# Loading the first slab in four parts and storing the middle slabs whole in a FiLM layer

## The chip, the cores and the metric

The kernel runs on one core of a Trainium2 chip. The metric is the device time of one execution in microseconds (us), lower is better. A core has a tensor engine (PE), a vector engine (DVE), a scalar engine (ACT), GpSimd (POOL) and a sync engine (SP). In this kernel SP and ACT issue the transfers, each to its own queue, and 16 DMA engines carry out both queues. The trace calls SP's queue q1 and ACT's q10. "SPq" and "ACTq" are the instruction streams of these engines where they issue transfers.

## The reference

```python
batch, seq, dim, cond_dim = 32, 512, 256, 64
gamma = conditioning @ gamma_proj            # [32, 64] @ [64, 256]
beta  = conditioning @ beta_proj
out   = x * (1 + gamma[:, None, :]) + beta[:, None, :]     # x, out: [32, 512, 256] float32
```

Two small products give each batch entry a scale and a shift for each of 256 features, and every one of the 512 sequence rows of that entry is scaled and shifted by them. x and out have 16.78 MB each, and each is moved once. Everything is float32.

## The kernel before

**Tiling.** x is seen as 4 slabs of 8 batch entries (4.19 MB). In a slab, partition p holds 32 consecutive rows of 256 features: 32 KB in one contiguous run, in HBM as in SBUF. So 16 neighbouring partitions belong to one batch entry, and each partition needs one row of gamma and one of beta. All four slabs have a tile of their own (`xs0` to `xs3`), which is updated in place and stored from; no buffer is used twice.

**Loads.** ACT first issues the three small loads: conditioning into `cond_s` (L48), gamma_proj and beta_proj into the two halves of `gbproj` (L50, L51). SP issues the loads of x (L59), in the order of the slabs, as the table `LOADS` (L38) says: slab 0 in two DMAs, of 8 and of 24 rows of each partition, every other slab in one DMA of 32 rows. A DMA of n rows consists of 128 runs of n KB, one for each partition.

**Scale and shift.** An identity repeated 16 times along its columns (`rident`, L67) is multiplied with conditioning (L72), which gives its transpose with each column repeated for the 16 partitions of a batch entry. It goes to SBUF (`cond_T`, L74). For each slab one product with `gbproj` (L79) gives gamma and beta for each partition in PSUM (`gb_p`). ACT copies them to SBUF as `gb_s`, with 1 added to gamma (L82, L85).

**The main loop.** It runs over the slabs, and in a slab over two groups of 16 rows. DVE takes 11 rows of a group and reads gamma and beta from PSUM: L100 does (gamma + 1) * x, L103 adds beta. POOL takes the other 5 rows and reads the SBUF copies: L102 multiplies, L104 adds. When both have finished with a group, ACT issues its store (L105), 16 rows of each partition, 2.10 MB. The tile framework places the semaphores, and orders each engine's instructions; POOL runs the multiplications of both groups of slab 0 before its additions.

**Order.** Each engine works through its instructions in order, and each of the two DMA queues takes its transfers in the order of issue. The stores stand on ACT behind the copies to `gb_s`.

Of the kernel before, what the change touches and what calls it, by code (L numbers as in the profile page):

```python
# [2 lines left out]

# [5 lines left out]


@with_exitstack
def kernel(
    ctx: ExitStack,
    tc: tile.TileContext,
    x: bass.AP,
    conditioning: bass.AP,
    gamma_proj: bass.AP,
    beta_proj: bass.AP,
    out: bass.AP,  # L20
):
    nc = tc.nc
    f32 = mybir.dt.float32
    ALU = mybir.AluOpType

    batch, seq, dim = x.shape
    cond_dim = conditioning.shape[1]
    P = 128
    SLABS = 4
    BS = batch // SLABS  # L30
    REP = P // BS
    ROWS = BS * seq // P
    assert SLABS * BS == batch and REP * BS == P and ROWS * REP == seq

    x_v = x.flatten_outer_dims().rearrange("(s p r) d -> s p r d", s=SLABS, p=P)
    o_v = out.flatten_outer_dims().rearrange("(s p r) d -> s p r d", s=SLABS, p=P)

    LOADS = {0: [8, 24]}  # L38
    GROUP = 16
    ON_DVE = 11  # L40

    consts = ctx.enter_context(tc.tile_pool(name="consts", bufs=1))
    xpool = ctx.enter_context(tc.tile_pool(name="xpool", bufs=1))
    psum = ctx.enter_context(tc.tile_pool(name="psum", bufs=1, space=bass.MemoryType.PSUM))


    cond_s = consts.tile([batch, cond_dim], f32)
    nc.scalar.dma_start(out=cond_s, in_=conditioning)  # L48
    gbproj = consts.tile([cond_dim, 2 * dim], f32)
    nc.scalar.dma_start(out=gbproj[:, :dim], in_=gamma_proj)  # L50
    nc.scalar.dma_start(out=gbproj[:, dim:], in_=beta_proj)  # L51

    slabs = []
    for s in range(SLABS):
        xs = xpool.tile([P, ROWS, dim], f32, name=f"xs{s}")
        slabs.append(xs)
        r = 0
        for n in LOADS.get(s, [ROWS]):
            nc.sync.dma_start(out=xs[:, r : r + n, :], in_=x_v[s, :, r : r + n, :])  # L59
            r += n  # L60
        assert r == ROWS


    ident = consts.tile([batch, batch], f32)
    make_identity(nc, ident)
    rident = consts.tile([batch, batch * REP], f32)
    nc.vector.tensor_copy(  # L67
        out=rident.rearrange("p (b g) -> p b g", g=REP),
        in_=ident.to_broadcast([batch, batch, REP]),
    )  # L70
    cond_T_p = psum.tile([cond_dim, batch * REP], f32)
    nc.tensor.matmul(cond_T_p, lhsT=cond_s, rhs=rident, start=True, stop=True)  # L72
    cond_T = consts.tile([cond_dim, batch * REP], f32)
    nc.vector.tensor_copy(out=cond_T, in_=cond_T_p)  # L74

    gb_p, gb_s = [], []
    for s in range(SLABS):
        p_t = psum.tile([P, 2 * dim], f32, name=f"gb_p{s}")
        nc.tensor.matmul(p_t, lhsT=cond_T[:, s * P : (s + 1) * P], rhs=gbproj,  # L79
                         start=True, stop=True)  # L80
        s_t = consts.tile([P, 2 * dim], f32, name=f"gb_s{s}")
        nc.scalar.activation(out=s_t[:, :dim], in_=p_t[:, :dim],  # L82
                             func=mybir.ActivationFunctionType.Identity,
                             bias=1.0, scale=1.0)
        nc.scalar.copy(out=s_t[:, dim:], in_=p_t[:, dim:])  # L85
        gb_p.append(p_t)
        gb_s.append(s_t)

    def rows(t, n):
        return bass.AP(tensor=t.tensor, offset=t.offset, ap=[t.ap[0], [0, n], t.ap[1]])  # L90

    for s in range(SLABS):
        xs = slabs[s]
        g_p, b_p = gb_p[s][:, :dim], gb_p[s][:, dim:]
        g_s, b_s = gb_s[s][:, :dim], gb_s[s][:, dim:]
        for r0 in range(0, ROWS, GROUP):
            v = xs[:, r0 : r0 + ON_DVE, :]
            w = xs[:, r0 + ON_DVE : r0 + GROUP, :]
            nv, nw = ON_DVE, GROUP - ON_DVE
            nc.vector.scalar_tensor_tensor(out=v, in0=rows(g_p, nv), scalar=1.0, in1=v,  # L100
                                           op0=ALU.add, op1=ALU.mult)
            nc.gpsimd.tensor_tensor(out=w, in0=w, in1=rows(g_s, nw), op=ALU.mult)  # L102
            nc.vector.tensor_add(out=v, in0=v, in1=rows(b_p, nv))  # L103
            nc.gpsimd.tensor_tensor(out=w, in0=w, in1=rows(b_s, nw), op=ALU.add)  # L104
            nc.scalar.dma_start(out=o_v[s, :, r0 : r0 + GROUP, :],  # L105
                                in_=xs[:, r0 : r0 + GROUP, :])


# [1 line left out]
_INS = ['x', 'conditioning', 'gamma_proj', 'beta_proj']  # L110
_OUTS = [((32, 512, 256), 'float32')]


# [23 lines left out]
```

## Time and profile before

| | |
|---|---|
| Median of 5 runs | 84.53 us (84.29 to 84.71) |
| The profiled execution | 84.53 us, its span 82.7 us |
| DVE busy | 49.9 us (60%) |
| POOL busy | 46.2 us (56%) |
| PE, ACT busy | 9.1 us, 3.9 us |
| Moved by DMA | 33.69 MB, mean 407 GB/s over the span |
| Small loads to landing | cond 3.2 us, gamma 9.2 us, beta 13.0 us |
| Eight stores to landing | 18.8 us, the median from issue |

The span runs from the first instruction of the core to the last; the rest of the time lies outside it. The busy shares are those of the engines. The page also has two rows in 40 equal slices, for the engines and for the DMA engines, in tenths (9 is 90% or more). In a row of a DMA queue the columns are packets, MB, and the time of the packets as a share of 16 engines in the stretch that was asked for. A packet is counted in the stretch in which it starts, so that shares of short stretches can be a little over 100%. In this kernel a packet of x is one run of one partition: the loads of 8, 24 and 32 rows have packets of 8, 24 and 32 KB.

### The profile page before, as it was taken

The numbers are of one execution on the slowest core, as the hardware profiler recorded it, in microseconds if no ns is written. First come the engines' busy times: TensorE is split into PE (matmuls) and PEld (weight loads), VectorE is DVE, ScalarE is ACT, GpSimd is POOL, SyncE is SP. The second block draws the span as 40 slices with busy tenths as digits, with TensorE's granted clock in tenths as the row PEclk, the third lists the DMA queues.
The fourth block names the chain that finished last, engine by engine and source line by source line (L and its number), as shares of the span: only waits on it lengthen the run. The fifth ranks groups of instructions, "written<-read, shape, count | busy, mean of one in ns | idle before, by whom it ended". The sixth has DMA issues, their size and how long they took to land.

```text
span 82.7 us, 156 instructions
## 1 busy us (share of the span) xinstructions
PE 9.1 (11%) x10; PEld 2.8 (3%) x10; DVE 49.9 (60%) x18; ACT 3.9 (5%) x9; POOL 46.2 (56%) x22
## 2 busy tenths in 40 slices
PE   0090000899600000000000000000000000000000
PEld 0000000443000000000000000000000000000000
DVE  2002000049999999999999999999999920000000
ACT  0600000034400000000000000000000000000000
POOL 2000000059999999999999999999995000000000
DMA  2899999989969989898989969999999999999992
GB/s 48 309 543 396 388 396 523 396 364 507 507 285 475 507 364 380 364 523 380 396 380 507 491 285 467 404 451 436 412 452 404 451 436 412 452 404 459 428 412 95
DMA packets 2080, 33.69 MB, mean 407 GB/s; under 512 B 288, under 2 KB 416, under 8 KB 416
## 3 DMA queue, kind: packets, MB, share of 16 engines
q1 hardware_dynamic: 720, 16.78, 48.6%
q10 hardware_dynamic: 1360, 16.92, 47.9%
HBM read 16.92 MB, written 16.78 MB: 407 GB/s over the span
## 4 chain that ended last, share of the span: by engine, by line
DVE 48%; DMA 16%; issue 11%; PE 2%; ACTq 1%; ACT 1%
DVE xs L100 30%; DVE xs L103 19%; DMA gbproj<-in_beta_proj_dram 16%; PE gb_p L79 2%; ACTq L50 1%; ACTq L48 0%; ACT gb_s L82 0%; ACT gb_s L85 0%
## 5 line engine op out<-in xcount | busy, mean ns | idle before, releaser
L102 POOL TENSOR_TENSOR xs<-xs,gb_s 128x1280 f32<-128x1280 f32 x8 | 23.0, 2889 | 16.3 <-ACT gb_s L82 16.3
L100 DVE SCALAR_TENSOR_TENSOR xs<-gb_p,xs 128x2816 f32<-128x2816 f32 x8 | 24.7, 3084 | 10.9 <-ACT gb_s L85 10.9
L103 DVE TENSOR_TENSOR xs<-xs,gb_p 128x2816 f32<-128x2816 f32 x8 | 24.7, 3087 | 0.3
L104 POOL TENSOR_TENSOR xs<-xs,gb_s 128x1280 f32<-128x1280 f32 x8 | 23.0, 2890 | 0.0
L79 PE MATMUL gb_p<-gbproj,cond_T 64*128 64x512 f32 x8 | 7.2, 1073 | 8.9 <-DMA gbproj<-in_beta_proj_dram 8.9
L74 DVE COPY cond_T<-cond_T_p 64x512 f32<-64x512 f32 x1 | 0.7, 683 | 4.5 <-PE cond_T_p L72 4.5
L79 PEld LDWEIGHTS gb_p<-gbproj,cond_T 64*128 64x128 f32 x8 | 2.5, 326 | 13.6 <-issue 13.6
L72 PE MATMUL cond_T_p<-rident,cond_s 32*64 32x512 f32 x2 | 1.9, 1065 | 4.1 <-DMA cond_s<-in_conditioning_dram 4.1
L82 ACT ACTIVATE gb_s<-gb_p 128x256 f32<-128x256 f32 x4 | 1.5, 384 | 16.5 <-PE gb_p L79 16.5
L85 ACT COPY gb_s<-gb_p 128x256 f32<-128x256 f32 x4 | 1.5, 366 | 0.0
L82 ACT ACT_TABLE_LOAD x1 | 1.3, 1283 | 2.4 <-issue 2.4
L67 DVE COPY rident<-ident 32x512 f32<-32x512 f32 x1 | 0.4, 415 | 1.2 <-POOL ident masks.py:199 1.2
L72 PEld LDWEIGHTS cond_T_p<-rident,cond_s 32*64 32x64 f32 x2 | 0.3, 202 | 4.0 <-issue 4.0
masks.py:197 POOL MEMSET ident<- 32x32 f32 x1 | 0.1, 114 | 0.3 <-POOLq L121 0.3
masks.py:199 POOL TENSOR_SCALAR_AFFINE_SELECT ident<-ident 32x32 f32<-32x32 f32 x1 | 0.2, 203 | 0.1
L121 POOL MEMSET const-float32-0.0<- 128x1 f32 x1 | 0.1, 104 | 0.2 <-issue 0.2
L121 POOL MEMSET const-bfloat16-1.0<- 128x1 bf16 x1 | 0.1, 107 | 0.0
L121 POOL MEMSET const-uint8-127<- 128x1 uint8 x1 | 0.1, 107 | 0.0
L121 POOL MEMSET const-float32-1.0<- 128x1 f32 x1 | 0.1, 104 | 0.0
## 6 DMA issues: line engine op xcount, KB each, us to landing
out_dram<-xs ACTq DMA_DIRECT2D x8, 2048.0 KB, 18.8
xs<-in_x_dram SPq DMA_DIRECT2D x3, 4096.0 KB, 33.1
xs<-in_x_dram SPq DMA_DIRECT2D x1, 3072.0 KB, 12.4
xs<-in_x_dram SPq DMA_DIRECT2D x1, 1024.0 KB, 4.8
gbproj<-in_gamma_proj_dram ACTq DMA_DIRECT2D x1, 64.0 KB, 9.2
gbproj<-in_beta_proj_dram ACTq DMA_DIRECT2D x1, 64.0 KB, 13.0
cond_s<-in_conditioning_dram ACTq DMA_DIRECT2D x1, 8.0 KB, 3.2
```

The lines of the kernel that those rows point to most:

```text
L50: nc.scalar.dma_start(out=gbproj[:, :dim], in_=gamma_proj)
L67: nc.vector.tensor_copy(out=rident.rearrange("p (b g) -> p b g", g=REP), in_=ident.to_broadcast([batch, batch, REP]),)
L72: nc.tensor.matmul(cond_T_p, lhsT=cond_s, rhs=rident, start=True, stop=True)
L74: nc.vector.tensor_copy(out=cond_T, in_=cond_T_p)
L79: nc.tensor.matmul(p_t, lhsT=cond_T[:, s * P : (s + 1) * P], rhs=gbproj, start=True, stop=True)
L82: nc.scalar.activation(out=s_t[:, :dim], in_=p_t[:, :dim], func=mybir.ActivationFunctionType.Identity, bias=1.0, scale=1.0)
L85: nc.scalar.copy(out=s_t[:, dim:], in_=p_t[:, dim:])
L100: nc.vector.scalar_tensor_tensor(out=v, in0=rows(g_p, nv), scalar=1.0, in1=v, op0=ALU.add, op1=ALU.mult)
L102: nc.gpsimd.tensor_tensor(out=w, in0=w, in1=rows(g_s, nw), op=ALU.mult)
L103: nc.vector.tensor_add(out=v, in0=v, in1=rows(b_p, nv))
L104: nc.gpsimd.tensor_tensor(out=w, in0=w, in1=rows(b_s, nw), op=ALU.add)
L121: nc = _bacc.Bacc("TRN2", target_bir_lowering=False, num_devices=1)
```

## The change

Two tables of the kernel are changed, and the store at the end of the loop follows the new one.

- `LOADS` gives slab 0 four DMAs of 8 rows each, where it had one of 8 and one of 24. SP issues seven loads of x and not five.
- `STORES` gives the rows at which a slab's stores end. Slabs 0 and 3 are stored in two halves as before. Slabs 1 and 2 are stored by one DMA of 32 rows, 4.19 MB, after their second group. ACT issues six stores and not eight.

The lines that issue the three small loads are not touched. The arithmetic, its groups and its split between DVE and POOL are the same.

```diff
-    LOADS = {0: [8, 24]}
+    LOADS = {0: [8, 8, 8, 8]}
+    STORES = {0: (16, 32), 1: (32,), 2: (32,), 3: (16, 32)}
     GROUP = 16
     ON_DVE = 11
...
             nc.gpsimd.tensor_tensor(out=w, in0=w, in1=rows(b_s, nw), op=ALU.add)
-            nc.scalar.dma_start(out=o_v[s, :, r0 : r0 + GROUP, :],
-                                in_=xs[:, r0 : r0 + GROUP, :])
+            done = r0 + GROUP
+            if done in STORES[s]:
+                e0 = 0
+                for e1 in STORES[s]:
+                    if r0 < e1 <= done or STORES[s] == (ROWS,):
+                        nc.scalar.dma_start(out=o_v[s, :, e0:e1, :], in_=xs[:, e0:e1, :])
+                    e0 = e1
```

## The prediction

> **What bounds the kernel now.** I read the page first: engine shares, the row of DMA busy tenths, the queues.
>
> ```profile
> span 82.7 us, 156 instructions
> PE 9.1 (11%) x10; PEld 2.8 (3%) x10; DVE 49.9 (60%) x18; ACT 3.9 (5%) x9; POOL 46.2 (56%) x22
> DMA  2899999989969989898989969999999999999992
> q1 hardware_dynamic: 720, 16.78, 48.6%
> q10 hardware_dynamic: 1360, 16.92, 47.9%
> ```
>
> DVE and POOL are busy for a little over half the span. The 16 DMA engines have no empty slice between the first and the last, and the two queues' shares add to 96.5%. Queue q1 carries the x loads from SP; q10 carries the stores and the three small loads from ACT (16.92 MB is 16.78 of stores and 0.14 of small loads).
>
> Next the chain of waits, the timeline and the DMA issues, to see whether compute could be what ends last.
>
> ```profile
> 1.72 13.04 DMA gbproj<-in_beta_proj_dram
> 17.43 2.90 POOL L102 TENSOR_TENSOR xs<-xs,gb_s 128x1280 f32<-128x1280 f32 x1 [16.30 <-ACT gb_s L82]
> 26.07 0.37 ACTq L105 DMA_DIRECT2D out_dram<-xs  x1
> 30.06 0.34 ACTq L105 DMA_DIRECT2D out_dram<-xs  x1
> 66.80 0.34 ACTq L105 DMA_DIRECT2D out_dram<-xs  x1
> out_dram<-xs ACTq DMA_DIRECT2D x1, 2048.0 KB, 15.1
> ```
>
> The chain names beta's load (13.04 us), which holds back all arithmetic until 17.4 us. That chain is true for DVE, but DVE does not set the end. The last store is issued at 66.80 and lands 15.1 us later, at 81.9. One store of 2.10 MB needs about 4.9 us of the engines (64 packets of 0.61 us per engine make eight stores: 39 us), so some 10 us of that are a queue of earlier stores. The end is set by bytes over DMA rate: an earlier start of the arithmetic buys nothing unless the DMA engines would have been empty.
>
> So the price list is that of the packets. I asked for the DMA view in stretches with one kind of packet each: 3 to 4.7 us (8 KB loads), 5.2 to 9.5 (24 KB loads beside gamma), 15.12 to 22.3 (32 KB loads), 50 to 80 (16 KB stores), 28.4 to 33.8 (loads and stores). The columns are packets, MB, share of 16 engines.
>
> ```profile
> q1 hardware_dynamic: 86, 0.70, 97.7%
> ...
> q1 hardware_dynamic: 64, 1.57, 85.8%
> q10 hardware_dynamic: 64, 0.07, 4.3%
> ...
> q1 hardware_dynamic: 96, 3.15, 101.4%
> ...
> q10 hardware_dynamic: 881, 12.86, 100.1%
> ...
> q1 hardware_dynamic: 48, 1.57, 77.1%
> q10 hardware_dynamic: 32, 0.52, 22.6%
> ```
>
> Share times 16 engines times the stretch, over packets, gives one packet on one engine: 8 KB 0.309 us; 24 KB 0.922; 32 KB 1.213; 16 KB stores 0.612 (of the 881, 96 are 4-byte completion packets, which I leave out). Per KB they are 0.0386, 0.0384, 0.0379 and 0.0383: within 2%. The row of loads and stores together is the exception: between 28.4 and 33.8 us a 32 KB load took 0.771 x 16 x 5.4 / 48 = 1.388 us, while the stores beside it kept 0.612. That dip cost (1.388 - 1.213) x 48 / 16 = 0.5 us per engine.
>
> **The change, part by part.** The sum is made against the profiled execution: 84.53 us with a span of 82.7, so 1.8 us lie outside. It equals the median of the five runs (84.53; 84.29 to 84.71). A change under about 0.3%, 0.25 us, can't be told from none.
>
> *Slab 0 as four loads of 8 rows instead of 8 and 24.* Each engine carries 8 partitions, one packet each: 8 packets of 8 KB and 8 of 24 KB become 32 of 8 KB. Added: 24 x 0.309 = 7.42 us. Removed: 8 x 0.922 = 7.38. Net +0.04. This lies on the path, as all DMA time does. SP issues two more DMAs, 0.36 to 0.43 us each in the trace (one took 0.70); the engines have the first 8-row load to work on from 1.7 us and need 2.5 us for each, so the issues are hidden. If that cover were gone, 0.4 us each would show.
>
> A rule speaks against this part. The Trainium skill, "DMA: Bandwidth & Descriptors", section Bandwidth, gives 341 GB/s for a 1 MB transfer measured alone and 425 for 16 MB, and its fit charges about 2.0 us fixed per DMA. Two more DMAs would be +4 us by that (an estimate from the page). The trace differs: the 3 to 4.7 us row moves 0.70 MB of 8 KB loads at 97.7% of the engines, and the seam between slab 0's two loads, at 4.8 us, lies in the third slice of the page's DMA row, which reads 9. With the next load already queued the fixed part is covered, so I charge 0.04 and not 4; the page's price would hold only if SP came late.
>
> *The small loads.* The diff does not move their issue: cond, gamma and beta still leave ACT at 0.74, 1.17 and 1.72. What changes is what they alternate with. In the 5.2 to 9.5 row, 64 x packets go with exactly 64 gamma packets: one for one. Gamma and beta have 4 packets per engine and a completion each, so ten turns. A turn costs 0.92 + 0.05 us beside 24 KB packets and 0.31 + 0.05 beside 8 KB ones. From about 5 us, ten turns of 0.36 bring beta home near 9 us (my estimate, 7 to 9.5), not 14.76. POOL and DVE then start near 11.8 instead of 17.5. The bytes are the same, so on the path this is worth 0; its cover is the DMA queue itself.
>
> *Slabs 1 and 2 stored whole.* For these slabs 32 packets of 16 KB per engine become 16 of 32 KB. No row shows a 32 KB store. The bounds are twice the 16 KB one (1.224) and the load of that size (1.213): 0 to -0.17 us. Halfway, -0.08. ACT issues two DMAs fewer (0.34 us each), hidden, as ACT has nothing else by then. Each whole store waits for both halves of its slab, so the first half goes out some 6 us later (DVE's four 3.09 us instructions per slab). Queued behind it on ACT are only the stores of later slabs, which are ready later anyway.
>
> *Does the queue run dry?* This is what would break the sum. With slab 0 starting near 11.8, its two stores issue near 20.3 and 24.3 (8.6 and 12.6 us after POOL's start, as in the timeline). Before, q10 has no packet from 28.4 to 29.7 us, so the first store packet came about 3.7 us after its issue at 26.07; now writing begins near 24. From there each engine alternates 32 KB loads with 16 KB stores; before, from 34.5 to 49 us, this ran at about 287 and 142 GB/s (4.16 and 2.06 MB in 14.5 us). Slab 2 has about 0.65 MB by then; the other 3.5 MB at 287 GB/s bring it home near 36.5, and 4.2 MB more bring slab 3 home near 51 (before, the last load landed 39.3 us after its issue at 10.43, so at 49.7). Slab 1 landed 21.6 us after its issue at 1.63, and does so again. DVE, at 12.25 us a slab, ends slab 0 at 24.2, slab 1 at 36.4, slab 2 at 48.8, slab 3 at 63.3. When loads end, the store queue still holds the tail of slab 0 and all of slab 1; slab 2 joins at 48.8. At 4.9 us per 2.1 MB these last to about 71, while slab 3's halves are ready at 59.7 and 63.3. That leaves about 8 us of margin after the 3.7 us. What is late next is nothing.
>
> Sum: +0.04 - 0.08 = -0.04 us. 84.53 - 0.04 = 84.5.
>
> **The rivals.**
>
> *The mixed stretch costs more (slower).* The only large loss of before is the dip of 0.5 us, in loads, just as the first store joined them. If reading slab 2 while writing slab 0 is what costs, it now lasts longer: before, three load packets per engine met it; now slab 0's writing covers the last six or seven. At 0.175 us each that is +0.5 to +0.7 us: 85.1. It decides from two more slow packets per engine (0.35 us). For it: the slow loads appear together with the stores. Against it: from 34.5 us on loads and stores ran together at full pace, and store packets were never slow; the five runs' spread of 0.42 us is as large as such a dip, so it may be chance.
>
> *The dips go (faster).* A smaller one is the first round of slab 1, at 12.5 to 13.9 us, when packets of 32 KB took some 1.34 us. If these dips belong to the old order of transfers (24 KB runs, first stores at 29.8 us), up to 0.6 us comes back: 83.9. Against it: nothing in the trace names a cause.
>
> *A load issued late (slower).* The fifth x load was held 7.6 us by gamma:
>
> ```profile
> SPq L59 <- DMA gbproj<-in_gamma_proj_dram: 7.6, 1, 7.6
> ```
>
> A completion counter is used again there. Seven x loads now need more of them, and a wait of slab 2's load is bounded by the landings ahead of it. If slab 2's load waited for slab 1's landing (about 23 us) the engines would empty at 22 and refill about 1 us after the issue: +2 us, 86.6. It decides from a release after 22 us. Against it: a counter of an early, small transfer is the natural one to come free, and gamma was. And that the change does nothing as its words say (no small load is moved on its queue) gives the forecast's time again.
>
> **How the numbers follow.** Unchanged within 0.3%: 0.46. Mixed stretch: 0.27. Dips gone: 0.22. Late load: 0.05. So faster 0.22, same 0.46, slower 0.32; the likeliest time is 84.5, its own range 84.25 to 84.8. To 8 in 10 I take in most of the first two rivals: 83.95 to 85.3. The late load and the outer part of the dips stay out.
>
> **What would show it.** Right: beta landing near 9 us and the arithmetic starting near 12, yet the end near 81.9; DMA tenths of 8 and 9 throughout; six stores, the last issued near 63 and landing some 18 us later instead of 15.1. Packets of 0.309 us for 8 KB, and 1.21 to 1.22 for the 32 KB stores. The first rival: load packets of 1.4 us over more of 24 to 37 us. The second: no such stretch. The third: an empty slice near 22 us and a wait of SP on a load of x. Wrong altogether: a slice under 8 tenths late in the span, before the last store is issued.

## The result, and the profile after

The changed kernel takes 84.05 us (median of 27 runs, 83.90 to 85.62) against 84.53 us (48 runs). The ratio is 0.9962, with a 95% interval of 0.9948 to 0.9975: faster by 0.25 to 0.52%. A second set of runs, with runs of before beside them, gave 0.9942 (0.9914 to 0.9969). Of the kernels below, those with stores of 8 rows, two loads of 16, one delay and the other slab order were profiled in a disturbed execution, so their load packets are not read here.

The page of the changed kernel, first the span and the DMA rows, then the issues with their time to landing:

```profile
span 83.0 us, 155 instructions
DMA  3899999979969999896999989799699979899980
q1 hardware_dynamic: 1008, 16.78, 48.2%
q10 hardware_dynamic: 1072, 16.92, 47.6%
...
out_dram<-xs ACTq DMA_DIRECT2D x2, 4096.0 KB, 23.9
gbproj<-in_beta_proj_dram ACTq DMA_DIRECT2D x1, 64.0 KB, 7.6
```

The DMA engines are full from end to end, as before. Beta lands after 7.6 us instead of 13.0. The profiled execution took 84.78 us, more than the median and more than before, with a span 0.3 us longer than before's 82.7. A wrong conclusion is easy here. Share times span gives the time an engine spends on packets, on average over the 16: 40.0 us of loads and 39.5 of stores after, 40.2 and 39.6 before. The engines had less to do, yet the end came later: the last store issued at 65.58 and landed 16.6 us later, at 82.2, and one engine's completion packet is the only DMA packet after 81.5 us. In the second profile of the same kernel (84.33 us) nothing is left after 81.5. One late engine sets the end of an execution, so the sums over all 16 engines are a steadier guide than the span.

The timeline after, for the answer to the lines of before:

```profile
20.64 0.37 ACTq L111 DMA_DIRECT2D out_dram<-xs  x1
24.63 0.34 ACTq L111 DMA_DIRECT2D out_dram<-xs  x1
38.10 3.09 DVE L101 SCALAR_TENSOR_TENSOR xs<-gb_p,xs 128x2816 f32<-128x2816 f32 x1 [1.31 <-DMA xs<-in_x_dram]
53.16 3.09 DVE L101 SCALAR_TENSOR_TENSOR xs<-gb_p,xs 128x2816 f32<-128x2816 f32 x1 [2.73 <-DMA xs<-in_x_dram]
65.58 0.34 ACTq L111 DMA_DIRECT2D out_dram<-xs  x1
out_dram<-xs ACTq DMA_DIRECT2D x1, 2048.0 KB, 16.6
```

The stores start 5.4 us earlier than before. DVE now waits for slabs 2 and 3, 1.31 and 2.73 us in brackets, which costs nothing: the last store still waits behind others, 16.6 us where its own bytes need 4.9.

Where the time came from is in the load packets where the stores join. The rows of one stretch, 23 to 38 us, are, in order: before, after, after a second time.

```profile
q1 hardware_dynamic: 160, 4.72, 76.3%
...
q1 hardware_dynamic: 144, 4.19, 65.7%
...
q1 hardware_dynamic: 146, 4.23, 66.6%
```

MB over 32 KB gives the 32 KB packets: 144, 128 and 129 (the rest of the count are completion packets). An undisturbed one takes 1.213 us. Before, an engine spent 0.763 x 15 = 11.45 us on 9 packets that should take 10.92: 0.53 us too much. After, the same working gives 0.15 and 0.21. So 0.3 to 0.4 us of slow loads are gone, most of the gain of 0.3 to 0.5 us.

A smaller stretch of slow loads is gone too, the first round of slab 1. Here are its rows, before from 12.5 to 13.0 us, then after from 12.7 to 13.4:

```profile
q1 hardware_dynamic: 32, 0.52, 269.1%
q10 hardware_dynamic: 30, 0.03, 18.2%
...
q1 hardware_dynamic: 36, 0.56, 185.6%
```

Both hold 16 packets of 32 KB, besides completion packets and, after, four packets of 8 KB. They took 1.34 us each before and 1.21 after, which is 0.12 us less per engine. Before, beta's last packets (q10) are still under way; after, beta has landed by then. Of the kernels below, stores alone and beta behind slab 0 also have beta under way there, and their first round took 1.32 and 1.39 us. In loads alone, and with gamma and beta early, beta has landed, and it took 1.21.

The slow packets do not stand in one place even in the changed kernel. The rows of 23.1 to 27 us and of 27 to 36 us are, for the first profile and then for the second:

```profile
q1 hardware_dynamic: 32, 1.05, 64.8%
q1 hardware_dynamic: 80, 2.62, 67.9%
...
q1 hardware_dynamic: 32, 1.05, 62.3%
q1 hardware_dynamic: 80, 2.62, 69.5%
```

A load packet took 1.26 and then 1.22 us in the first, 1.21 and then 1.25 us in the second, though the first store packet came at 24.1 and 24.8 us.

### The profile page after: what moved, and what is told of

It reads as the page before. It is cut to its first block, busy times and chain, and to the rows that moved or that the text cites. A ratio compares the mean times of both kernels' runs of the same rounds, so it can differ in the third digit from the quotient of the medians.

```text
span 83.0 us, 155 instructions
## 1 busy us (share of the span) xinstructions
PE 9.1 (11%) x10; PEld 2.8 (3%) x10; DVE 50.1 (60%) x18; ACT 3.9 (5%) x9; POOL 46.3 (56%) x22
## 4 chain that ended last, share of the span: by engine, by line
DMA 62%; DVE 15%; ACTq 1%; issue 0%; DVEq 0%
DMA xs<-in_x_dram 53%; DMA gbproj<-in_beta_proj_dram 9%; DVE xs L104 7%; DVE xs L101 7%; ACTq L51 1%; ACTq L49 0%; DVEq L101 0%
```

## The experiments

Theory A said that fewer and longer store packets gained, B that the loads gained, through the slow load packets where the stores join, C that it was spread. Each ratio is to runs of before made beside it.

**Loads alone.** Against the changed kernel:

```diff
-    STORES = {0: (16, 32), 1: (32,), 2: (32,), 3: (16, 32)}
+    STORES = {s: (16, 32) for s in range(SLABS)}
```

> Slab 0 in four loads of 8 rows, all slabs stored in halves as before. Theory A (fewer, longer store packets are what gained): no gain here, +0.04 us by the prediction's packet prices, 84.5 to 84.6. Theory B (the loads gained: beta lands near 9.3 us, the stores begin near 24 us instead of 29.8, and the stretch of slow loads at that point shrinks): most of the 0.48 us, 84.0 to 84.2, with the load packets between 23 and 29 us near 1.25 us instead of 1.39. Theory C (the gain is spread of runs): ratio between 0.998 and 1.002 here and in the store-only kernel.

Its load row in 23 to 38 us:

```profile
q1 hardware_dynamic: 144, 4.19, 65.6%
```

That is 0.14 us of slow loads, as after: the mechanism of B. The time did not follow at once: the ratio was 0.9984 (0.9945 to 1.0022), inconclusive; the profiled execution took 84.36 us. Its end shows a cost of another kind. Its last store lands at 64.33 + 17.2 = 81.5 us, 0.4 earlier than before, but its span ends 1.05 us after that, where before and after need 0.8. The end of the program, line L138, between 81.5 and 81.9 us, in this kernel:

```profile
64.33 0.34 ACTq L111 DMA_DIRECT2D out_dram<-xs  x1
out_dram<-xs ACTq DMA_DIRECT2D x1, 2048.0 KB, 17.2
L138 SPq EVENT_SEMAPHORE  x5: 27/28/24274, 57.3 to 81.8; - x5
```

SP checks one completion counter after another, and not in the order of landing. Here one wait, begun at 57.3, lasts 24.3 us until the last store's landing, and four more checks follow, the last at 81.8. In the changed kernel the last store has the counter that is checked last, and none follows. So the number of DMAs moves the end by some 0.2 us through the counter that the last store happens to get. Taken off, loads alone keep the 0.4 us that their last landing gained; that subtraction is argued from the trace, not timed.

**Stores alone.**

```diff
-    LOADS = {0: [8, 8, 8, 8]}
+    LOADS = {0: [8, 24]}
```

> Slab 0 loaded as before (8 and 24 rows), slabs 1 and 2 stored whole. Theory A: most of the gain, 84.0 to 84.2. Theory B: the packets alone, some -0.1 us (32 KB stores at 1.213 us for two of 0.612 less their gaps, 16 per engine), 84.4 to 84.5, with the slow loads at 28.4 to 33.8 us as before. Theory C: within 0.2% of before.

Load row of 23 to 38 us, and the page's store queue:

```profile
q1 hardware_dynamic: 160, 4.72, 77.7%
...
span 83.0 us, 153 instructions
q10 hardware_dynamic: 1072, 16.92, 47.5%
```

0.74 us of slow loads: the dip is still there. The stores' packets take 0.475 x 83.0 = 39.4 us against 39.6: the -0.1 to -0.2 us that the packet prices give, and no more. Two closing checks behind the last landing, 0.06 us each, take most of that back here. The ratio was 1.0007 (0.9982 to 1.0032). Theory A falls: most of the gain is not in the stores, though their 0.1 to 0.2 us is part of it in the changed kernel, where no check follows.

**The changed kernel again**, with no edit.

> The changed kernel once more, for a second profile and for the spread: its first profiled execution (84.78 us) lay above its median (84.05), with the last store landing on the engines over 81.1 to 82.2 us. If that lag of one engine is what parts the upper from the lower runs, a profile of 84.0 us lands its last store within some 0.4 us and shows fewer slow load packets; if the lower runs start earlier instead, the first packet comes before 1.7 us. Median 83.9 to 84.2 by all theories but C, which has 84.3 to 84.6.

Median 84.43 us beside 84.79 of before in that session, ratio 0.9942 as told above. C falls. The profile of 84.33 us starts its packets when before did and lacks the late engine. It lies in the middle of its runs, so what parts the upper from the lower runs stays open.

**Stores of 8 rows**, with loads as before:

```diff
-                        nc.scalar.dma_start(out=o_v[s, :, e0:e1, :], in_=xs[:, e0:e1, :])
+                        for e in range(e0, e1, 8):
+                            nc.scalar.dma_start(out=o_v[s, :, e:e + 8, :], in_=xs[:, e:e + 8, :])
```

> Loads as before; each store of 16 rows is issued as two of 8 rows, so that every store packet has 8 KB and there are 16 stores. Doubles the suspected price of store packets the other way. Theory A (the length of store packets matters beyond its row): at least as much lost as the two whole stores gain over half of the bytes, +0.5 to +1 us, 85.0 to 85.5. Theory B: packets at 0.309 for half of 0.612 give 64 x 0.006 = +0.4 us, 84.9, or less if the gap behind a packet is part of these numbers. Theory C has no say.

Ratio 1.0023 (0.9987 to 1.0059). The +0.6 to +1.2% of A is not there, which again speaks against it. Whether the 0.4 us of the packet prices is there can't be said from this interval.

The next question was why the slow loads shrink. B1: it is the moment at which the stores join. B2: it is the 24 KB packets of slab 0.

**Gamma and beta early, 24-row load kept.** The stores are halves, as before; against the kernel before:

```diff
-    nc.scalar.dma_start(out=gbproj[:, :dim], in_=gamma_proj)
-    nc.scalar.dma_start(out=gbproj[:, dim:], in_=beta_proj)
...
             r += n
+            if (s, r) == (0, 8):
+                nc.sync.dma_start(out=gbproj[:, :dim], in_=gamma_proj)
+                nc.sync.dma_start(out=gbproj[:, dim:], in_=beta_proj)
```

> Slab 0 in 8 and 24 rows as before, stores in halves as before; gamma and beta are issued by SP between the two loads of slab 0, so they land near 6 us and the first store packet comes near 21 us instead of 29.8. Theory B1 (the slow loads come with the moment at which the stores join, and cost by what the loads are at then; the length of the first packets has no part): the dip of 28.4 to 33.8 us is gone from its place; at 21 us, where the last packets of slab 1 are under way as the last of slab 2 were before, it is either as deep (0.5 us per engine) or, if an early join is cheap, under 0.25. Theory B2 (the 24 KB packets themselves make it): 0.5 us of slow loads wherever the stores join, 84.5. By B1 with a cheap early join 84.0 to 84.2.

Ratio 1.0113 (1.0070 to 1.0155): clearly slower. The design was poor: group 0 needs rows 0 to 15, thus the 24-row load too, so the stores joined at 26.4 us and not at 21. The row of 23 to 38 us:

```profile
q1 hardware_dynamic: 148, 4.26, 68.7%
```

130 packets, 0.45 us too much. By its slow loads, a join between those of after (24 to 25 us) and before (29.8) is already dear. Yet they are not what makes this kernel slower, as before has more of them. One or a few engines were late, with packets left after 81.6 us.

**Beta behind slab 0, and beta inside slab 1.** Both keep 8 KB packets for slab 0 and store in halves, as loads alone; beta is issued by SP later.

```diff
-    nc.scalar.dma_start(out=gbproj[:, dim:], in_=beta_proj)
...
             r += n
+            if (s, r) == (0, 32):
+                nc.sync.dma_start(out=gbproj[:, dim:], in_=beta_proj)
```

> Slab 0 in four loads of 8 rows, stores in halves, but beta is issued by SP behind the last load of slab 0: it lands near 13 us and the stores join near 28 us, in the middle of slab 2, instead of 24.8. B1: the dip moves to about 27 to 33 us and is deeper than the 0.13 to 0.2 us of the loads-only and the changed kernel, 0.3 to 0.5. B2: it stays at 0.2 or less, since all packets of slab 0 have 8 KB.

The second has `1: [8, 24]` in `LOADS` and `(1, 8)` in the condition:

> As the one with beta behind slab 0, but slab 1 is loaded in 8 and 24 rows with beta between them: it lands near 15.3 us and the stores join near 30.3 us, late in slab 2, about where they join in the kernel before. B1: a dip of 0.5 us per engine at 29 to 34 us as before, 84.5 or more. B2: 0.2 us or less, as slab 0 has 8 KB packets; if 24 KB packets anywhere count, it can't tell, and the one with beta behind slab 0 decides.

Their load rows of 23 to 38 us, in this order:

```profile
q1 hardware_dynamic: 159, 4.69, 76.5%
...
q1 hardware_dynamic: 160, 4.72, 75.8%
```

0.63 us (143 packets, join at 28.5) and 0.45 us (144 packets, join at 31.0). The ratios are 1.0040 (1.0021 to 1.0060) and 1.0061 (1.0044 to 1.0078). B2 falls with the first: slab 0 has no packet over 8 KB, and the dip is as deep as before. Most of the lost time is not the dip but the end of the program. Line L139 from 81.9 to 82.4 us in the first and from 81.8 to 82.2 in the second:

```profile
L139 SPq EVENT_SEMAPHORE  x5: 28/28/29099, 53.0 to 82.3; - x5
...
L139 SPq EVENT_SEMAPHORE  x6: 17/28/28, 81.9 to 82.2; - x6
```

In the first the long wait ends with the last landing and four checks follow; in the second the first of six does, and five follow. At 0.06 us each that is 0.24 and 0.3 us, out of the 0.3 and 0.4 us by which their medians exceed that of before.

**Two loads of 16 rows**, `LOADS = {0: [16, 16]}`, stores in halves.

> Slab 0 in two loads of 16 rows, all else as before: gamma and beta take turns with 16 KB packets (0.61 us), beta lands near 11.8 us and the stores join near 26.8 us. B1: slow loads of 0.2 to 0.4 us, between the 0.13 to 0.2 of a join at 24.8 and the 0.5 to 0.7 of one at 29.8; 84.2 to 84.4. B2: as before if long packets make it, as after if only those of 24 KB do.

Ratio 0.9985 (0.9971 to 0.9998), beside 0.9962 for the change: a smaller gain, as B1 wants. Whether its slow loads lie between the two, its packets can't show.

**Gamma and beta early with 8-row loads:** the changed kernel with the edit of gamma and beta above. It was also the candidate for a version that beats both.

> The changed kernel, with gamma and beta issued by SP behind the first 8 rows: both land near 6 us, the arithmetic starts near 9 us, and the stores join near 21.5 us, in the last packets of slab 1. Theory B1 (when the stores join sets the slow loads: cheap at 24.8, 0.13 to 0.20 us per engine; dear at 28.5 and later, 0.45 to 0.7): an earlier join is cheap too, 0.2 or less, median 83.8 to 84.1. Theory B3 (small transfers in SP's own queue hold up the loads, whatever the join): deep as in the three kernels that had beta on SP, 0.4 or more, 84.4 to 84.7.

Ratio 1.0069 (1.0037 to 1.0101): slower, no better version. The first store was issued at 15.87 us, so the join moved to 20.5 us, into the last packets of slab 1. The rows of 13 to 22.4 us, this kernel first, then before:

```profile
q1 hardware_dynamic: 98, 3.18, 84.3%
...
q1 hardware_dynamic: 116, 3.74, 92.0%
```

97 packets in 0.843 x 9.4 = 7.92 us: 0.57 us too much. Before has 0.01 there, as its stores join later. The dip follows the join. But "early is cheap" fails, or the join is not all that counts: at 20.5 us it is dear, at 24 to 25 cheap, from 26.4 on dear. B3, that small transfers in SP's own queue hold up the loads, had forecast this dip, and nothing here rules it out.

The slow loads do not explain the lost time. Over both queues, share times span is 79.7 us here and 79.8 in before, and the profiled execution took 84.58 us, no more than before. It is one of the two shortest of eight; what made the others up to 0.9 us longer is not shown.

Where the slow loads begin is seen best here. From 17.4 to 20.4 us no store packet has started yet, and the only row is that of the loads:

```profile
q1 hardware_dynamic: 32, 1.05, 99.8%
```

That is 1.50 us for each packet of 32 KB.

**One and two multiplications by ones ahead of the first group**, in the changed kernel:

```diff
+    ones = consts.tile([P, dim], f32)
+    nc.scalar.activation(out=ones, in_=gb_p[0][:, :dim],
+                         func=mybir.ActivationFunctionType.Identity, bias=1.0, scale=0.0)
...
+            if s == 0 and r0 == 0:
+                for _ in range(1):     # 2 in the second kernel
+                    nc.vector.tensor_mul(out=v, in0=v, in1=rows(ones, nv))
+                    nc.gpsimd.tensor_tensor(out=w, in0=w, in1=rows(ones, nw), op=ALU.mult)
```

> The changed kernel, its transfers untouched, with one multiplication by ones on DVE and on POOL put ahead of the first group: the stores join some 3.3 us later, near 28 us, with everything else the same. B1: slow loads of 0.4 to 0.6 us per engine at 27 to 33 us, and the gain over before is gone, 84.4 to 84.6. B3: they stay at 0.2 or less, and the time at 84.0 to 84.2, since beta stays on ACT.

> As with one, but two multiplications by ones on each engine: the stores join near 31 us, a little later than in the kernel before (29.8). B1: 0.4 to 0.7 us of slow loads at 29 to 35 us, 84.4 to 84.6. B3: 0.2 or less, 84.0 to 84.2. The added 6 us of DVE lie under the queue of stores (8 us of margin by the prediction's working), so they should not show themselves; if they do, the last store is issued with DMA engines idle.

Both missed their aim. The tile of ones came last on ACT, and POOL took the second group first, so the first stores were issued at 31.98 and 37.43 us, far later than planned. With one delay the ratio was 1.0096 (1.0079 to 1.0113). With two it was 1.0773 (1.0746 to 1.0800), and the profile shows why the prediction's margin mattered. Stretches of that kernel; the last two columns are the DMA share and GB/s:

```profile
54.00:57.00 3.00, 0.00 (x0) 0.00 (x0) 3.00 (x2) 0.00 (x0) 3.00 (x2) 1.00 0.48 208
57.00:66.00 9.00, 0.00 (x0) 0.00 (x0) 9.00 (x4) 0.00 (x0) 9.00 (x5) 1.00 1.00 430
66.00:69.00 3.00, 0.00 (x0) 0.00 (x0) 3.00 (x2) 0.00 (x0) 3.00 (x2) 1.00 0.26 109
```

The engines stand idle for 0.52 x 3 + 0.74 x 3 = 3.8 us while DVE and POOL work without a pause. The stores of the first slabs are done, and nothing goes out until a whole slab is. So the whole stores are free only while the arithmetic is ahead. The loads were slow as well. From 14 to 40 us, before the stores joined, 304 packets took 1.36 us each:

```profile
q1 hardware_dynamic: 336, 9.96, 99.4%
...
68.07 0.34 ACTq L119 DMA_DIRECT2D out_dram<-xs  x1
```

But they do not set the end. From its first multiplication at 17.60 us DVE waits for no load, and slab 2's whole store is issued at 68.07 us, when the arithmetic is done with it. From there slabs 2 and 3 are still to be stored, 4 x 4.9 = 19.6 us, and the last store landed at 88.9. With faster loads the engines would only have stood idle longer before 68.07.

The same count covers one delay, where DVE waits for no load either and this store is issued at 62.62 us. The last landing can then not come before 82.2 us, 0.3 later than before's, and would come some 1.2 us later still if the queue is empty, as with two delays. That makes 84.8 to 86.0 us (an estimate), with 85.3 measured: the late store can account for the loss, and the kernel says nothing on B1 or B3.

**Another order of slabs**, 0, 1, 3, 2, in the kernel before:

```diff
-    for s in range(SLABS):
-        xs = slabs[s]
+    for s in ORDER:               # [0, 1, 3, 2], for the loads too
+        xs = slabs[s]
```

> The kernel before with its slabs loaded, computed and stored in the order 0, 1, 3, 2: the stores of slab 0 join while slab 3 is being read and not slab 2. Theory B4 (the slow loads come from the addresses of what is read and written together): the 0.5 us dip at 28.4 to 33.8 us changes clearly, below 0.25 or above 0.8. B1: it stays at 0.45 to 0.75 and the time within 0.2% of before.

Ratio 0.9999 (0.9985 to 1.0014). Reading slab 3 in place of slab 2 when the stores of slab 0 join changes nothing in the time, which speaks against B4; the dip itself can't be read in its profile.

## Why the prediction was right or wrong

The bound was right: the DMA engines are full throughout, and the start of the arithmetic at 12.0 us instead of 17.4 was worth nothing by itself. The likeliest time, 84.5, was 0.45 too high. The measured 84.05 lies in the range, near the case of the dips gone (83.9, chance 0.22).

- *Four loads of 8 rows, +0.04 us.* Right in size. In the changed kernel from 9 to 11.5 us, a stretch with a seam between two loads, 130 packets of 8 KB took 0.310 us each and filled 100.8% of the engines. The 2 us per DMA of the page's rule do not appear. The Trainium skill, "DMA: Bandwidth & Descriptors", section Anatomy of one DMA, fits these 2 us on DMAs issued from GpSimd, and the loads here are issued from SP.
- *Small loads.* Beta landed at 1.72 + 7.6 = 9.3 us, foretold near 9. One for one with 8 KB packets was the right model.
- *Whole stores, 0 to -0.17, taken at -0.08.* A 32 KB store took 0.996 x 16 x 8 / 105 = 1.214 us, the lower end; all stores together 0.1 to 0.2 us less. In the time of stores alone it is below what can be told.
- *The queue never dry.* Right for this kernel. Slabs 2 and 3 landed 1.5 and 2 us later than worked out, so the last store was issued at 65.6 and not near 63; the queue of stores covered it. Two delays showed that the margin has an end.
- *The late load* did not come about: loads 6 and 7 were released at 5.6 and 9.3 us.
- *The step that failed* is what was left out of the sum: the dip of 0.5 us stayed in the forecast unchanged. It shrank to 0.15 to 0.21, and the smaller one of 0.12 us at slab 1's first round went. That the time lies in the range is owed to the rival and not to the sum. I had a rival for it becoming longer with a longer mixed stretch, which was wrong, and one for its going, with too little chance. That second rival named the first stores at 29.8 us and the 24 KB runs as its possible causes. The first led to the right place, since the deep dips lie where the stores join; the second was not it.

The shown part, in packets and with one profile for each kernel (two for the changed one): loads alone shrink the slow loads, stores alone do not, and the deep dips lie where the stores join. In times it is not shown, since loads alone was inconclusive. What stays open is why the join of after is cheap. An early join was dear too, so the moment alone doesn't order the cases. The three kernels with gamma or beta on SP that joined at 26.4 us or later, and the one at 20.5, were all dear; but so were before and stores alone, which have them on ACT. A delay of the stores with the transfers untouched would have parted these, but the kernels made for it missed their moment.

## What to carry to other kernels

Where the DMA engines are full, an earlier start of the arithmetic is worth nothing by itself; price each packet and look for stretches in which a packet takes longer than its kind does elsewhere, because only those can move. Check at each store that is made larger whether the queue behind it still holds work until it is ready. With changes of half a per cent, compare packet times over all engines as well as times: here a late engine or the order of the closing checks was as large as the effect.

## What the runs showed of the hardware

- Where the first stores came in, loads slowed down, by 0.14 (loads alone) to 0.74 us (stores alone) per engine in all; in before this lasted about 5 us. The stores beside them did not: 0.61 us for 16 KB in that stretch of before, as later without loads.
- The slowing can begin before the first store packet. In the one with gamma and beta early and 8-row loads, the store issued at 15.87 us has no packet up to 20.4 us, and the loads from 17.4 us on took 1.50 us. In the kernel before it starts after 28.4 us, with a first store packet after 29.7.
- In slab 1's first round, loads of 32 KB took 1.32 to 1.39 us in the three kernels in which beta was still under way, and 1.21 in those in which it had landed.
- The closing checks of the completion counters cost 0.06 us each behind the last landing, some 0.2 us in loads alone and 0.3 with beta inside slab 1.
